# Attention kernel: q's norm factor given to the sigmoids as their scale, and the root's steps and all scaling of k on GpSimd

## The chip, the core and the metric

The kernel runs on one core of one Trainium2 chip. A core has five engines with a queue of instructions each: TensorE (PE in the profile; PEld is its weight load), VectorE (DVE), ScalarE (ACT), GpSimd (POOL) and SyncE (SP, which issues the DMAs here). An engine works its queue strictly in order; engines wait for one another through semaphores. The metric is the device time of one execution in microseconds; of several runs the median is taken.

## The reference

One block of an encoder on 1024 frames of 1024 features, all in float32: a SwiGLU feed-forward (half weight), stick-breaking attention, and a second SwiGLU. Only the attention is touched by the change.

```python
qkv = (xn @ w_qkv).reshape(b, s, 3, SB_HEADS, SB_HEAD_DIM)     # 16 heads of 64
q = rms_norm(qkv[:, :, 0], q_gain)...                          # over the 64 of a head
k = rms_norm(qkv[:, :, 1], k_gain)...
z = jnp.einsum('bhqd,bhkd->bhqk', q[:, :, lo:hi], k[:, :, :hi]) * scale      # scale = 1/8
log_beta = jax.nn.log_sigmoid(z)
log_1m = jnp.where(mask, jax.nn.log_sigmoid(-z), 0.0)
rev = lax.cumsum(log_1m, axis=3, reverse=True)                 # the keys between s and t
w = jnp.where(mask, jnp.exp(log_beta + rev_excl), 0.0)
outs.append(jnp.einsum('bhqk,bhkd->bhqd', w, v[:, :, :hi]))
```

`rms_norm` multiplies a head's 64 values of one frame by r = 1/sqrt(mean of squares + 1e-6) and by the gain. For q, r is one number for each frame and head, so it is one number for each row of z.

## The kernel before

Frames are stored in reverse order, so that the cumulative product runs forward. Matrix products are made of parts: every operand is split into a high part (rounded by ScalarE) and a low part (the rest, a subtraction), and three products are summed; this split is the helper on lines 159 and 160 and appears in the profile under these lines.

**Tiling.** The 16 heads are worked in 8 pairs. `qkv(p)` is a sequence of 8 steps, one for each block of 128 frames: a step makes q, k and v of a pair's two heads in one bank of PSUM (24 products of 128 x 384), copies q and k into a tile `qk`, takes squares and their sums (`ssq`), and splits v. After the fourth and the eighth step (a *half* of the frames: half 1 comes first, then half 0) the root r is found for 4 blocks x 4 (two q heads, two k heads) at once, in `rsqrt`: a first guess from the bits of the number and three rounds of Newton, on tiles of 128 x 16. Then q and k of that half are multiplied by r.

**Per head.** `prep` turns q and k of a half with PE transposes, puts in the gains and splits them (`q_s`, `kh_s`, `kl_s`). `weights` makes, for each block of 128 queries, z = q·k in banks of 512 keys (PE, lines 729 and 730), two sigmoids of each bank on ScalarE (`om`, line 731: sigmoid of -z; `w`, line 732: sigmoid of z; the factor 0.125 is the sigmoid's scale), a cleared first column (GpSimd, line 733), a scan that multiplies up `om` (VectorE, line 734), and the product of the two (line 735). `values` turns the weights back with PE transposes (line 756), splits them into `th` (ScalarE) and `tl` (VectorE), and multiplies them by v into the bank `bo` (lines 765 and 766); `o` is put together on lines 768 and 769. There are two `om` buffers, so that the sigmoids of a block wait until the product of line 735 two blocks before has read its `om`; there is one buffer of `w` for each block.

**Engines.** Which engine does an elementwise step is written in a set of names, `ON_POOL`: w0, w4 and w5 (the product of line 735 for query blocks 0, 4 and 5: 1023, 511 and 383 columns) are on GpSimd, the other five on VectorE; k of half 1 is scaled on GpSimd, k of half 0 and all of q on VectorE; of the four splits of a pair's qkv weights (`wql`, 128 x 768 each) three are on GpSimd and the second one on VectorE.

**Order.** The program is written in a fixed order (`PLAN`, a list of prep and use for head and half; `FILLS`, which says after which query block a qkv step of the *next* pair is put in; the values of a use come one use later), and a scheduler with priorities (`sooner`) turns it into one queue for each engine. So in a pair's stretch of the queues stand its own weights and values and the qkv steps of the next pair.

**Memory.** A kernel's tiles come from pools that are laid one after another in the order in which they are named; what follows the attention uses the same memory, so its loads and splits wait for the attention's tiles. Pool `sq` holds the squares, their sums and the root's tiles.

Of the kernel before, what the change touches and what calls it, by code (L numbers as in the profile page):

```python
# [9 lines left out]
F32 = mybir.dt.float32  # L10
# [3 lines left out]
ALU = mybir.AluOpType  # L14
# [20 lines left out]
ON_POOL = {  # L35
    "k1", "last w5", "last w7", "w0", "w4", "w5", "wo0", "wo1", "wo2", "wo3", "wql0", "wql2", "wql3", "xl0",
    "xl2", "xl3", "xl4",
}
# [59 lines left out]
def macaron_kernel(ctx, tc, x, g1, w1_in, w1_out, gm, w_qkv, gq, gk, w_o, g2, w2_in, w2_out, out):  # L98
# [8 lines left out]
    def lane(name):  # L107

        return pool_e if name in ON_POOL else dve
# [32 lines left out]
    def any_bank(tags=ROUND):  # L142
        turn[0] += 1
        return bank(tags[turn[0] % len(tags)])

    ident = cpool.tile([P, P], F32, name="ident")
    make_identity(nc, ident)

    below = cpool.tile([P, 16], F32, name="below")
    xh = cpool.tile([P, KD, T], F32R, name="xh")  # L150
# [7 lines left out]
    def split(raw, hi, lo, engine=None):  # L158
        act.activation(hi, raw, AF.Copy)  # L159
        (engine or dve).tensor_tensor(lo, raw, hi.bitcast(F32), op=ALU.subtract)  # L160

    def rsqrt(pool, ss, inv_n):

        shape = list(ss.shape)
        a = pool.tile(shape, F32, name="rs_a")
        u = pool.tile(shape, F32, name="rs_u")
        y = pool.tile(shape, F32, name="rs_y")
        dve.tensor_scalar(a, ss, inv_n, EPS, op0=ALU.mult, op1=ALU.add)
        dve.tensor_scalar(y.bitcast(I32), a.bitcast(I32), -0.5, -550020641.0, op0=ALU.mult, op1=ALU.add)
        for _ in range(3):  # L170
            dve.scalar_tensor_tensor(out=u, in0=y, scalar=0.5, in1=a, op0=ALU.mult, op1=ALU.mult)
            dve.tensor_tensor(u, u, y, op=ALU.mult)
            dve.scalar_tensor_tensor(out=y, in0=u, scalar=1.5, in1=y, op0=ALU.subtract, op1=ALU.mult)
        return y
# [445 lines left out]
    with pools(  # L620
        "raw_qkv", "wq1", "wq0", "wq2", "qk1", "qk0", "vst0", "sq", "vst1", "st1", "st0", "om", "w", "first", "th", "o"
    ) as pl:
# [9 lines left out]
        def qkv_weights(p):  # L632
            wh, wl = {}, {}
            for k0 in (4, 0) if p == 0 else (0, 4):
# [15 lines left out]
        def qkv(p, state):  # L650
# [3 lines left out]
            for half in (1, 0):  # L654
# [4 lines left out]
                for i, tb in enumerate(b4):  # L659
# [3 lines left out]
                    with sooner(OFF["e"]):  # L663
                        sq = pl["sq"].tile([P, 4, DH], F32, name="sq")
                        act.activation(qk[:, i, 0:2].rearrange("p a b -> p (a b)"), ps[:, :P], AF.Copy)
# [9 lines left out]
                        if i == 3:  # L675
                            r = rsqrt(pl["sq"], ssq.rearrange("p a b -> p (a b)"), 1.0 / DH)
# [3 lines left out]
                            lane(f"q{half}").tensor_tensor(qv, qv, rq, op=ALU.mult)  # L680
                            for hd in range(2):
                                kv = qk[:, :, 2 + 2 * hd : 4 + 2 * hd, :].rearrange("p a c b -> p a (c b)")
                                rk = r[:, :, 2 + hd : 3 + hd].to_broadcast([P, 4, P])
                                lane(f"k{half}").tensor_tensor(kv, kv, rk, op=ALU.mult)
                    yield
# [27 lines left out]
        def weights(state, hd, half, fill):  # L713

            w = []
            for tb in range(half * 4, half * 4 + 4):
                with sooner(OFF["w"]):
# [4 lines left out]
                    for kb in range(half, 2):  # L722
# [7 lines left out]
                        pe.matmul(z[:, : off + n], q, state["k", hd, kb][1][:, keys], start=False, stop=True)  # L730
                        act.activation(om[:, c0 : c0 + n], z[:, off : off + n], AF.Sigmoid, scale=-0.125)  # L731
                        act.activation(wt[:, c0 : c0 + n], z[:, off : off + n], AF.Sigmoid, scale=0.125)
                    pool_e.memset(wt[:, 0:1], 0.0)
# [196 lines left out]
```

## Time and profile before

| | |
|---|---|
| median of 3 runs | 2067.39 us (2066.3 to 2070.5) |
| the profiled execution's own time | 2066.78 us |
| its span, first to last instruction | 2064.9 us |
| granted TensorE clock, mean | 0.983 |
| busy in the span | PE 95%, PEld 80%, DVE 67%, ACT 47%, POOL 47% |
| the attention | from about 690 us to 1335 us of the span |
| a pair's period inside it | 75.3 us |

Busy shares are means over stages that have different limits: the two feed-forwards take some 1,420 us and the attention some 645 us. Only the attention's rows say what this change can do. In a timeline row the first two numbers are start and duration in us, and the bracket at the end tells how long the engine had been idle and what ended it. Times inside a pair repeat every 75.3 us, so one pair is read and then multiplied.

### The profile page before, as it was taken

How to read it: one execution, taken by the hardware profiler on the slowest of the kernel's cores; microseconds unless marked ns; L12 is line 12 of the kernel's file. 1: busy time of each engine (PE TensorE's matmuls, PEld its weight loads, DVE VectorE, ACT ScalarE, POOL GpSimd, SP SyncE). 2: the span in 40 equal slices, each digit the busy share in tenths (PEclk: the TensorE clock that was granted, in tenths of full speed). 3: DMA queues.
4: the chain of work that ended last, by engine and by line, in shares of the span. 5: the costliest groups of instructions: out<-in, count | busy, mean ns of one | idle time of the engine just before them, and what ended most of it. 6: DMA issues, size and time to landing. Idle time of an engine off the chain costs nothing.

```text
span 2064.9 us, 27122 instructions
## 1 busy us (share of the span) xinstructions
PE 1956.6 (95%) x9624; PEld 1649.9 (80%) x9624; DVE 1377.0 (67%) x1840; ACT 965.4 (47%) x1876; POOL 966.3 (47%) x772
## 2 busy tenths in 40 slices
PE   7899999999999989899899997899999999999999
PEld 6788888887887878777787785588888888888887
DVE  7845546447749688889888889638556455447754
ACT  6433433433335366667666666425333434434332
POOL 2567666655546132322322324102466666655554
PEclk9999999999999999999999997899999999999999
DMA  5223323249886111001001103322233232259974
GB/s 199 72 92 123 102 83 127 97 142 322 318 287 216 55 31 41 24 19 41 29 14 41 47 6 102 121 88 72 82 104 106 97 117 98 95 175 339 332 259 160
DMA packets 163031, 251.85 MB, mean 122 GB/s; under 512 B 10960, under 2 KB 80592, under 8 KB 162896
## 3 DMA queue, kind: packets, MB, share of 16 engines
q1 hardware_dynamic: 162896, 250.13, 35.3%
q8 instruction: 75, 1.23, 0.2%
q14 instruction: 60, 0.49, 0.1%
HBM read 193.99 MB, written 56.10 MB: 121 GB/s over the span
## 4 chain that ended last, share of the span: by engine, by line
PE 72%; DVE 18%; ACT 3%; issue 2%; POOL 2%; DMA 1%; ACTq 0%; DVEq 0%; POOLq 0%
PE ka L244 6%; PE ka L245 6%; PE ka L246 5%; DVE om L734 4%; PE kc L246 4%; PE kc L244 4%; PE kc L245 4%; PE kb L246 3%; PE kb L244 3%; PE kb L245 3%; PE ma L244 3%; PE ma L246 3%; PE ma L245 3%; PE mb L245 3%; PE mb L244 3%; PE mb L246 3%
## 5 line engine op out<-in xcount | busy, mean ns | idle before, releaser
L160 POOL TENSOR_TENSOR u<-sf,u 128x512 fp32r<-128x512 f32 x160 | 226.5, 1417 | 160.5 <-ACT u L159 159.7
L160 POOL TENSOR_TENSOR rp<-raw,rp 128x1024 fp32r<-128x1024 f32 x84 | 207.8, 2477 | 180.3 <-ACT rp L159 172.4
L160 POOL TENSOR_TENSOR u<-raw,u 128x512 fp32r<-128x512 f32 x136 | 198.7, 1464 | 142.3 <-ACT u L159 142.1
L159 ACT ACTIVATE u<-sf 128x512 fp32r<-128x512 f32 x160 | 100.9, 630 | 217.7 <-PE kb L245 89.8
L352 DVE TENSOR_TENSOR h<-h 128x512 f32<-128x512 f32 x110 | 134.9, 1228 | 87.1 <-POOL h L453 86.4
L734 DVE TENSOR_TENSOR_SCAN om<-om,first 128x512 f32<-128x512 f32 (+7 forms) x128 | 186.3, 1458 | 3.0 <-ACT om L731 2.6
L159 ACT ACTIVATE rp<-rh 128x1024 fp32r<-128x1024 f32 (+1 forms) x78 | 76.8, 984 | 210.9 <-issue 68.8
L244 PE MATMUL ka<-xh,u 128*128 128x512 f32 (+1 forms) x448 | 162.8, 364 | 8.2 <-ACT s L402 7.6
L245 PE MATMUL ka<-xl,u 128*128 128x512 f32 (+1 forms) x448 | 162.4, 363 | 1.2 <-DVE xl L160 1.2
L246 PE MATMUL ka<-xh,u 128*128 128x512 f32 (+1 forms) x448 | 162.0, 362 | 0.0
L159 ACT ACTIVATE u<-raw 128x512 fp32r<-128x512 f32 x136 | 84.8, 632 | 160.7 <-PE ka L245 102.1
L474 DVE TENSOR_TENSOR raw<-raw 128x1024 f32<-128x1024 f32 (+1 forms) x60 | 94.2, 1573 | 96.0 <-DMA raw<-w_out 88.9
L244 PE MATMUL bq<-wqh,xh 128*128 128x384 f32 x448 | 156.9, 350 | 0.0
L245 PE MATMUL bq<-wql,xh 128*128 128x384 f32 x448 | 155.1, 346 | 0.0
L246 PE MATMUL bq<-wqh,xl 128*128 128x384 f32 x448 | 154.0, 344 | 0.0
L244 PE MATMUL ma<-rp 128*128 128x512 f32 x352 | 137.4, 390 | 2.9 <-DVE h L406 2.9
L379 DVE TENSOR_TENSOR sf<-raw 128x512 f32<-128x512 f32 x80 | 79.1, 990 | 89.2 <-POOL u L160 89.1
L246 PE MATMUL ma<-rp 128*128 128x512 f32 x352 | 137.0, 389 | 0.0
L245 PE MATMUL ma<-rp 128*128 128x512 f32 x352 | 137.0, 389 | 0.0
L453 POOL TENSOR_TENSOR h<-h,g 128x512 f32<-128x512 f32 x80 | 111.0, 1387 | 36.4 <-DVE h L406 32.8
L159 ACT ACTIVATE th<-bt 128x512 fp32r<-128x512 f32 x192 | 94.5, 506 | 67.8 <-PE bt L756 63.3
L160 DVE TENSOR_TENSOR rp<-rh,rp 128x1024 fp32r<-128x1024 f32 (+1 forms) x70 | 108.8, 1568 | 24.9 <-ACT rp L159 22.6
(226 smaller groups left out, 5613.2 us busy)
## 6 DMA issues: line engine op xcount, KB each, us to landing
raw<-w_out SPq DMA_DIRECT2D x120, 512.0 KB, 5.2
raw<-w_in SPq DMA_DIRECT2D x88, 512.0 KB, 3.6
k<-h SPq DMA_DIRECT2D x154, 256.0 KB, 2.0
rh<-k SPq DMA_DIRECT2D x64, 512.0 KB, 6.0
raw_qkv<-w_qkv SPq DMA_DIRECT2D x64, 192.0 KB, 2.9
x_keep<-x SPq DMA_DIRECT2D x32, 256.0 KB, 3.4
x<-x_keep SPq DMA_DIRECT2D x32, 256.0 KB, 5.6
raw<-w_out SPq DMA_DIRECT2D x24, 256.0 KB, 4.1
```

The lines of the kernel that those rows point to most:

```text
L159: act.activation(hi, raw, AF.Copy)
L160: (engine or dve).tensor_tensor(lo, raw, hi.bitcast(F32), op=ALU.subtract)
L244: pe.matmul(dst, ah, bh, start=start and i == 0, stop=False, skip_group_check=onto)
L245: pe.matmul(dst, ah, bl, start=False, stop=False, skip_group_check=onto)
L246: pe.matmul(dst, al, bh, start=False, stop=stop and i == n - 1, skip_group_check=onto)
L352: dve.tensor_tensor(src, hb[of[0]], hb[of[1]], op=getattr(ALU, of[2]))
L379: dve.tensor_tensor(f[n], x, y, op=op)
L453: pool_e.tensor_tensor(h, h, gs[k], op=ALU.mult)
L474: dve.tensor_tensor(w[0], w[0], w[1], op=getattr(ALU, W_OF[m][2]))
L734: dve.tensor_tensor_scan(om[:, :L], om[:, :L], first[:, :L], initial=0.0, op0=ALU.mult, op1=ALU.max)
```

## The change

1. **q isn't scaled.** The product of q with r is left out. Two rows of factors, 0.125 r and -0.125 r, are made for each half (`f`, two small GpSimd instructions), and each of the two sigmoids takes its row's factor as a scale from memory in place of a constant. Before, q had to wait for r ahead of its transposes; now the sigmoids do.
2. **The root.** VectorE keeps the first two steps (`rs_a`, `rs_y`). The three rounds of Newton go to GpSimd, as 1 + 3 x 4 instructions on 128 x 16 (VectorE did a round in 3).
3. **k.** ScalarE copies q and k with one instruction where it used two, without writing each k head twice. GpSimd scales k for both halves: head 1 is written twice from one copy in one instruction of 512 columns, head 0 in two of 256.
4. **Weight splits.** All four `wql` splits of a pair are on GpSimd; the second one was on VectorE.
5. **Places in memory.** `f` makes the pool `sq` larger by 256 bytes per partition; the pool is named last, so that every other pool of the attention lies 2560 bytes, 5 x 512, lower than before or where it was. `below` (64 bytes) is laid ahead of the identity matrix, which so begins 64 bytes later.

The rows below are queue entries: source line (of the version it stands in), operation, output<-inputs, columns; `w` is the weights tile of a query block, told by its columns (511 is block 4, 383 block 5).

GpSimd, around the end of a pair, where half 0 of the next pair is scaled and the next pair's first weights begin; before:

```order
L160 TENSOR_TENSOR wql<-raw_qkv,wqh 128x768 x2
L733 MEMSET w_9810 128x1
L760 MEMSET th 128x128
L761 MEMSET tl 128x128
L160 TENSOR_TENSOR wql<-raw_qkv,wqh 128x768
L733 MEMSET w_9890 128x1
L735 TENSOR_TENSOR w_9890<-w_9890,om 128x511
L733 MEMSET w_9900 128x1
L735 TENSOR_TENSOR w_9900<-w_9900,om 128x383
```

And in the change, the same place from the last round's end (the twelve steps ahead of it, behind the first two `wql` splits, are left out):

```order
L746 MEMSET w_9840 128x1
L177 TENSOR_TENSOR rs_y<-rs_u,rs_y 128x16
L686 TENSOR_TENSOR qk_9526<-qk_9526,rs_y 128x4x128
L693 TENSOR_SCALAR f_9837<-rs_y 128x8 x2
L689 TENSOR_TENSOR qk_9526<-qk_9526,rs_y 128x4x64 x2
L773 MEMSET th 128x128
L159 TENSOR_TENSOR wql<-raw_qkv,wqh 128x768
L774 MEMSET tl 128x128
L159 TENSOR_TENSOR wql<-raw_qkv,wqh 128x768
L746 MEMSET w_9920 128x1
L748 TENSOR_TENSOR w_9920<-w_9920,om 128x511
L746 MEMSET w_9930 128x1
```

The thirteen steps, two `f`, three scalings of k and one more `wql` split now stand ahead of the product of block 4.

VectorE, some 30 us later, in the first weights of half 0 (query blocks 0, 1, 2: scans of 1024, 896, 768); before:

```order
L734 SCALAR_TENSOR_TENSOR om<-om,first 128x1024
L674 TENSOR_REDUCE ssq<-sq 128x4
L769 TENSOR_TENSOR o_7873<-bo,o_tmp 64x512
L673 TENSOR_TENSOR vst<-bq,vst 128x128
L160 TENSOR_TENSOR wql<-raw_qkv,wqh 128x768
L734 SCALAR_TENSOR_TENSOR om<-om,first 128x896
L673 TENSOR_TENSOR vst<-bq,vst 128x128
L735 TENSOR_TENSOR w_8441<-w_8441,om 128x895
L674 TENSOR_REDUCE ssq<-sq 128x4
L734 SCALAR_TENSOR_TENSOR om<-om,first 128x768
```

And in the change:

```order
L747 SCALAR_TENSOR_TENSOR om<-om,first 128x1024
L782 TENSOR_TENSOR o_8738<-bo,o_tmp 64x512
L679 TENSOR_REDUCE ssq<-sq 128x4
L678 TENSOR_TENSOR vst<-bq,vst 128x128
L747 SCALAR_TENSOR_TENSOR om<-om,first 128x896
L748 TENSOR_TENSOR w_9309<-w_9309,om 128x895
L678 TENSOR_TENSOR vst<-bq,vst 128x128
L679 TENSOR_REDUCE ssq<-sq 128x4
L747 SCALAR_TENSOR_TENSOR om<-om,first 128x768
```

The split between the scans of blocks 0 and 1 is gone from this queue (it is the last `wql` row of GpSimd's above).

GpSimd, in the second head's first weights, where half 1 of the next pair is scaled; before:

```order
L735 TENSOR_TENSOR w_10334<-w_10334,om 128x511
L684 TENSOR_TENSOR qk_10097<-qk_10097,rs_y 128x4x128 x2
L733 MEMSET w_10378 128x1
L735 TENSOR_TENSOR w_10378<-w_10378,om 128x383
L733 MEMSET w_10388 128x1
```

And in the change (five of the thirteen steps stand ahead of these rows):

```order
L746 MEMSET w_10367 128x1
L174 TENSOR_TENSOR rs_u<-rs_y,rs_a 128x16
L748 TENSOR_TENSOR w_10367<-w_10367,om 128x511
L175 TENSOR_TENSOR rs_u<-rs_u,rs_y 128x16
L176 TENSOR_SCALAR rs_u<-rs_u 128x16
L177 TENSOR_TENSOR rs_y<-rs_u,rs_y 128x16
L174 TENSOR_TENSOR rs_u<-rs_y,rs_a 128x16
L175 TENSOR_TENSOR rs_u<-rs_u,rs_y 128x16
L176 TENSOR_SCALAR rs_u<-rs_u 128x16
L177 TENSOR_TENSOR rs_y<-rs_u,rs_y 128x16
L686 TENSOR_TENSOR qk_10127<-qk_10127,rs_y 128x4x128
L693 TENSOR_SCALAR f_10364<-rs_y 128x8 x2
```

Behind them stand the two scalings of 256 columns and then the product of block 5 (383 columns).

The diff, without the moved names of the pools and of `below`:

```diff
 ON_POOL = {
-    "k1", "last w5", "last w7", "w0", "w4", "w5", "wo0", "wo1", "wo2", "wo3", "wql0", "wql2", "wql3", "xl0",
-    "xl2", "xl3", "xl4",
+    "last w5", "last w7", "w0", "w4", "w5", "wo0", "wo1", "wo2", "wo3", "xl0", "xl2", "xl3", "xl4",
 }
...
-    def rsqrt(pool, ss, inv_n):
+    def rsqrt(pool, ss, inv_n, e=dve):
...
+        if e is pool_e:
+            e.tensor_scalar(a, a, 0.5, None, op0=ALU.mult)
         for _ in range(3):
-            dve.scalar_tensor_tensor(out=u, in0=y, scalar=0.5, in1=a, op0=ALU.mult, op1=ALU.mult)
-            dve.tensor_tensor(u, u, y, op=ALU.mult)
-            dve.scalar_tensor_tensor(out=y, in0=u, scalar=1.5, in1=y, op0=ALU.subtract, op1=ALU.mult)
+            if e is pool_e:
+                e.tensor_tensor(u, y, a, op=ALU.mult)
+                e.tensor_tensor(u, u, y, op=ALU.mult)
+                e.tensor_scalar(u, u, 1.5, None, op0=ALU.subtract)
+                e.tensor_tensor(y, u, y, op=ALU.mult)
+            else:
+                e.scalar_tensor_tensor(out=u, in0=y, scalar=0.5, in1=a, op0=ALU.mult, op1=ALU.mult)
+                e.tensor_tensor(u, u, y, op=ALU.mult)
+                e.scalar_tensor_tensor(out=y, in0=u, scalar=1.5, in1=y, op0=ALU.subtract, op1=ALU.mult)
...
-                    split(raw, h_[:, ks], l_[:, ks], lane(f"wql{k // 2}") if p else pool_e)
+                    split(raw, h_[:, ks], l_[:, ks], pool_e)
...
-                        act.activation(qk[:, i, 0:2].rearrange("p a b -> p (a b)"), ps[:, :P], AF.Copy)
-                        pk = ps[:, P : 2 * P].rearrange("p (a b) -> p a b", b=DH)
-                        pk = pk.unsqueeze(2).to_broadcast([P, 2, 2, DH])
-                        act.activation(qk[:, i, 2:6].rearrange("p (a c) b -> p a c b", c=2), pk, AF.Copy)
                         act.activation(sq.rearrange("p a b -> p (a b)"), ps[:, : 2 * P], AF.Square)
+                        act.activation(qk[:, i, 0:4].rearrange("p a b -> p (a b)"), ps[:, : 2 * P], AF.Copy)
...
-                            qv = qk[:, :, 0:2, :]
-                            rq = r[:, :, 0:2].unsqueeze(3).to_broadcast([P, 4, 2, DH])
-                            lane(f"q{half}").tensor_tensor(qv, qv, rq, op=ALU.mult)
-                            for hd in range(2):
-                                kv = qk[:, :, 2 + 2 * hd : 4 + 2 * hd, :].rearrange("p a c b -> p a (c b)")
-                                rk = r[:, :, 2 + hd : 3 + hd].to_broadcast([P, 4, P])
-                                lane(f"k{half}").tensor_tensor(kv, kv, rk, op=ALU.mult)
+                            rk = r[:, :, 3:4].unsqueeze(3).to_broadcast([P, 4, 2, DH])
+                            kv = qk[:, :, 3:4, :].to_broadcast([P, 4, 2, DH])
+                            pool_e.tensor_tensor(qk[:, :, 4:6, :], kv, rk, op=ALU.mult)
+                            for to in (3, 2):
+                                rk = r[:, :, 2:3].to_broadcast([P, 4, DH])
+                                pool_e.tensor_tensor(qk[:, :, to, :], qk[:, :, 2, :], rk, op=ALU.mult)
+                            f = state["f", half] = pl["sq"].tile([P, 2, 4, 2], F32, name=f"f{half}")
+                            for n, c in enumerate((0.125, -0.125)):
+                                pool_e.tensor_scalar(f[:, n], r[:, :, 0:2], c, None, op0=ALU.mult)
...
-                        act.activation(om[:, c0 : c0 + n], z[:, off : off + n], AF.Sigmoid, scale=-0.125)
-                        act.activation(wt[:, c0 : c0 + n], z[:, off : off + n], AF.Sigmoid, scale=0.125)
+                        for to, sign in ((om, 1), (wt, 0)):
+                            act.activation(
+                                to[:, c0 : c0 + n], z[:, off : off + n], AF.Sigmoid,
+                                scale=f[:, sign, tb % 4, hd : hd + 1],
+                            )
```

More of the change, by code (lines that the diff above doesn't have):

```diff
@@ L144, in any_bank @@
         return bank(tags[turn[0] % len(tags)])
+    below = cpool.tile([P, 16], F32, name="below")
     ident = cpool.tile([P, P], F32, name="ident")
     make_identity(nc, ident)
-    below = cpool.tile([P, 16], F32, name="below")
     xh = cpool.tile([P, KD, T], F32R, name="xh")
@@ L620, in macaron_kernel @@
     with pools(
-        "raw_qkv", "wq1", "wq0", "wq2", "qk1", "qk0", "vst0", "sq", "vst1", "st1", "st0", "om", "w", "first", "th", "o"
+        "raw_qkv", "wq1", "wq0", "wq2", "qk1", "qk0", "vst0", "vst1", "st1", "st0", "om", "w", "first", "th", "o", "sq"
     ) as pl:
@@ L675, in qkv @@
                         if i == 3:
-                            r = rsqrt(pl["sq"], ssq.rearrange("p a b -> p (a b)"), 1.0 / DH)
+                            r = rsqrt(pl["sq"], ssq.rearrange("p a b -> p (a b)"), 1.0 / DH, pool_e)
                             r = r.rearrange("p (a b) -> p a b", b=4)
-                            qv = qk[:, :, 0:2, :]
-                            rq = r[:, :, 0:2].unsqueeze(3).to_broadcast([P, 4, 2, DH])
-                            lane(f"q{half}").tensor_tensor(qv, qv, rq, op=ALU.mult)
-                            for hd in range(2):
-                                kv = qk[:, :, 2 + 2 * hd : 4 + 2 * hd, :].rearrange("p a c b -> p a (c b)")
-                                rk = r[:, :, 2 + hd : 3 + hd].to_broadcast([P, 4, P])
-                                lane(f"k{half}").tensor_tensor(kv, kv, rk, op=ALU.mult)
+                            rk = r[:, :, 3:4].unsqueeze(3).to_broadcast([P, 4, 2, DH])
[7 more added lines that the diff above has]
+                                pool_e.tensor_scalar(f[:, n], r[:, :, 0:2], c, None, op0=ALU.mult)
                     yield
@@ L715, in weights @@
             w = []
+            f = state["f", half]
             for tb in range(half * 4, half * 4 + 4):
```

## The prediction

> **What bounds the kernel now.** First the busy time of stretches inside the attention, 70 us each; the columns are start and end, PE, PEld, DVE, ACT, POOL, then the granted clock.
>
> ```profile
> 830.00:900.00 70.00, 64.66 (x373) 56.30 (x373) 60.49 (x100) 44.95 (x110) 21.68 (x34) 1.00 0.10 31
> 970.00:1040.00 70.00, 63.15 (x356) 54.70 (x355) 59.60 (x99) 43.29 (x110) 20.46 (x32) 0.98 0.10 31
> 975.00:980.00 5.00, 3.34 (x18) 2.39 (x17) 4.90 (x8) 3.19 (x10) 0.10 (x1) 0.97 0.07 19
> 980.00:985.00 5.00, 5.00 (x25) 4.90 (x24) 2.81 (x5) 1.25 (x3) 0.41 (x2) 0.69 0.00 0
> ```
>
> TensorE is the bound with 64 of 70 us, VectorE follows with 60, and GpSimd has 70% to spare. So relief of VectorE pays only at the few places where TensorE waits for it. After the wait at 975 to 980 the clock granted falls to 0.69 for 5 us, which loses another 0.31 x 5 = 1.5 us. The second view is TensorE's timeline over one pair; the bracket is its wait.
>
> ```profile
> 943.94 0.50 PE L766 MATMUL bo<-tl,vst 128*128 128x512 f32 x1 [0.69 <-DVE tl L160]
> 947.81 0.41 PE L729 MATMUL bz<-kh_s,q_s 128*128 128x384 f32 x1 [0.46 <-DVE q_s L700]
> 950.14 0.38 PE L766 MATMUL bo<-tl,vst 128*128 128x256 f32 x1 [0.65 <-DVE tl L160]
> 955.30 0.47 PE L765 MATMUL bo<-th,vst 128*128 128x512 f32 x1 [1.59 <-DVE o L769]
> 979.23 0.51 PE L766 MATMUL bo<-tl,vst 128*128 128x512 f32 x1 [1.66 <-DVE tl L160]
> 995.05 0.50 PE L766 MATMUL bo<-tl,vst 128*128 128x512 f32 x1 [0.86 <-DVE tl L160]
> 1002.11 0.50 PE L766 MATMUL bo<-tl,vst 128*128 128x512 f32 x1 [0.44 <-DVE tl L160]
> ```
>
> All are waits for VectorE. Place one, a pair's end, holds 0.69 + 0.46 + 0.65 + 1.59 = 3.39 us; place two, the first weights of half 0, 1.66 + 1.5 for the clock; place three, where half 1 is scaled, 0.86 + 0.44 = 1.30. Together 7.85 us a pair. The stage from 740 to 1250 us holds 510 / 75.3 = 6.8 pairs, so 53 us is all that relief of VectorE can bring.
>
> **What leaves VectorE.** Groups of 735 to 1330 us (busy us and mean ns stand behind the bar):
>
> ```profile
> L171 DVE SCALAR_TENSOR_TENSOR rs_u<-rs_y,rs_a 128x16 f32<-128x16 f32 x42 | 22.2, 529 | 0.9
> L173 DVE SCALAR_TENSOR_TENSOR rs_y<-rs_u,rs_y 128x16 f32<-128x16 f32 x42 | 13.2, 315 | 0.9
> L172 DVE TENSOR_TENSOR rs_u<-rs_u,rs_y 128x16 f32<-128x16 f32 x42 | 8.7, 207 | 0.7
> L160 DVE TENSOR_TENSOR wql<-raw_qkv,wqh 128x768 fp32r<-128x768 f32 x6 | 11.4, 1902 | 0.0
> L684 DVE TENSOR_TENSOR qk<-qk,rs_y 128x512 f32<-128x512 f32 x15 | 11.3, 788 | 0.0
> L680 DVE TENSOR_TENSOR qk<-qk,rs_y 128x512 f32<-128x512 f32 x14 | 10.0, 716 | 0.5
> ```
>
> That is 76.8 us over 14 halves or 7 pairs, 11 us a pair. But the steps of 16 columns need not last 529 ns:
>
> ```profile
> 913.72 1.28 POOL L735 TENSOR_TENSOR w<-w,om 128x511 f32<-128x511 f32 x1 [0.69 <-DVE rs_y L169]
> 913.74 1.29 DVE L171 SCALAR_TENSOR_TENSOR rs_u<-rs_y,rs_a 128x16 f32<-128x16 f32 x1
> 915.07 0.17 DVE L172 TENSOR_TENSOR rs_u<-rs_u,rs_y 128x16 f32<-128x16 f32 x1
> 952.40 0.95 DVE L734 TENSOR_TENSOR_SCAN om<-om,first 128x384 f32<-128x384 f32 x1
> 952.49 1.91 POOL L735 TENSOR_TENSOR w<-w,om 128x511 f32<-128x511 f32 x1 [1.46 <-DVE rs_u L172]
> ```
>
> A step takes 0.17 us alone. The one at 913.74 took 1.29 and ended with GpSimd's product of 913.72; conversely the product of 1.28 us took 1.91 when a scan had begun 0.09 us ahead of it. The two engines keep one another out, and who came first goes first. The Trainium skill has this as a rule ("SBUF — State Buffer", Who interferes with whom): a VectorE operation with two inputs in SBUF and a GpSimd operation that reads SBUF contend for an exclusive lock. The trace agrees by the rows above. So a step that moves to GpSimd trades its time on VectorE for waits behind scans, and bars VectorE while it runs.
>
> **What it costs on GpSimd.**
>
> ```profile
> L735 POOL TENSOR_TENSOR w<-w,om 128x127 f32<-128x127 f32 x2 | 0.9, 452 | 1.2 <-DVE om L734 1.2
> 916.78 3.21 POOL L684 TENSOR_TENSOR qk<-qk,rs_y 128x512 f32<-128x512 f32 x2 [1.78 <-DVE rs_y L173]
> 947.89 1.84 POOL L160 TENSOR_TENSOR wql<-raw_qkv,wqh 128x768 fp32r<-128x768 f32 x1 [2.32 <-ACT wqh L159]
> ```
>
> Products of 511 columns in 1.28 and of 127 in 0.452 give 2.16 ns a column and 0.18 us ahead; 16 columns are then 0.21 us (an estimate by the line through the two), and 13 steps 2.7 us. Below nothing it can't go, and 13 x 0.452 = 5.9 is the upper bound. k of a half costs 3.2 us at most (3.21 stands above for the same 2 x 512 columns) and 2.2 at least (2 x 512 columns by the line, 2 x 1.28 at most); the two `f` 0.4.
>
> *Place two.*
>
> ```profile
> 969.19 2.40 POOL L735 TENSOR_TENSOR w<-w,om 128x1023 f32<-128x1023 f32 x1 [2.02 <-ACT w L732]
> 970.32 2.09 DVE L160 TENSOR_TENSOR wql<-raw_qkv,wqh 128x768 fp32r<-128x768 f32 x1
> 972.33 2.01 DVE L734 TENSOR_TENSOR_SCAN om<-om,first 128x896 f32<-128x896 f32 x1
> 978.50 0.68 DVE L160 TENSOR_TENSOR tl<-bt,th 128x512 fp32r<-128x512 f32 x1
> ```
>
> The weight split leaves VectorE here. Its 2.09 us aren't won whole: the product on GpSimd ends at 969.19 + 2.40 = 971.59, and a scan of two SBUF inputs waits that long. It starts at 971.59 instead of 972.33, 0.74 us earlier, and so does everything behind it to `tl` at 978.50, for which TensorE waits 1.66. I take 0.74 and half of the clock's loss: -1.5 us a pair. Bounds: -3.2 (wait and dip go) and 0.
>
> *Place three.* VectorE loses the steps and the q scaling from 913.74 on (to 916.74 + 0.69, 3.7 us); the waits of 1.30 can go. Against it stands the GpSimd queue: thirteen steps, `f`, k and then the product of block 5.
>
> ```profile
> 916.74 0.69 DVE L680 TENSOR_TENSOR qk<-qk,rs_y 128x512 f32<-128x512 f32 x1
> 920.00 1.34 POOL L735 TENSOR_TENSOR w<-w,om 128x383 f32<-128x383 f32 x1
> ```
>
> Before, that product ended at 921.34. Now rows start at 913.72: the product of 511 (1.28), 2.7 + 0.4, k 2.2 to 3.2 and 1.0 to 1.3 for 383 columns end at 921.3 to 922.6 with no scan in the way. Scans of 384 and 256 columns fall there, at most 0.95 each (the row of 952.40 has 384). I take 0.6 from the middle of that and 0.4 for collisions, +1.0 of delay, against -1.3: -0.3 a pair; bounds -1.3 and, with 1.3 and both scans of delay, 3.2 - 1.3 = +1.9.
>
> *Place one.*
>
> ```profile
> 943.81 0.16 DVE L169 TENSOR_SCALAR rs_y<-rs_a 128x16 int32<-128x16 int32 x1
> 945.33 1.48 DVE L734 TENSOR_TENSOR_SCAN om<-om,first 128x640 f32<-128x640 f32 x1
> 950.09 0.81 DVE L735 TENSOR_TENSOR w<-w,om 128x639 f32<-128x639 f32 x1
> 951.20 1.21 DVE L734 TENSOR_TENSOR_SCAN om<-om,first 128x512 f32<-128x512 f32 x1
> 954.43 0.38 ACT L731 ACTIVATE om<-bz 128x256 f32<-128x256 f32 x1 [1.11 <-POOL w L733]
> ```
>
> The guess is there at 944.0. GpSimd then needs 2.7 + 0.4 + 2.2 to 3.2, then two splits of 1.84 and the product of 1.28: it ends at 954.3 to 955.3 without collisions, where it ended at 952.49 + 1.91 = 954.40. But the scans of 945.33, 951.20 and 952.40 and the product of 950.09 (1.48 + 1.21 + 0.95 + 0.81 = 4.45 us in all) bar the chain; between none and all I take half, so the product comes 0.4 + 2.2 = 2.6 us later. ScalarE's sigmoid at 954.43 waits for that product already, since there are two `om`, and behind it in its queue are `th` and the next head's sigmoids. VectorE without its steps can bring all of -3.4; against it +2.6: -0.8 a pair; bounds -3.4 and 0.4 + 4.5 - 3.4 = +1.5.
>
> Sum of the places: -1.5 - 0.3 - 0.8 = -2.6 a pair, x 6.8 = -17.7 us.
>
> *ScalarE.*
>
> ```profile
> L731 ACT ACTIVATE om<-bz 128x512 f32<-128x512 f32 x95 | 58.9, 621 | 8.6 <-PE bz L730 5.9 <-POOL w L735 2.0
> L699 ACT ACTIVATE kh_s<-bz,gk_sb 128x512 fp32r<-128x512 f32 x30 | 20.9, 696 | 7.2 <-PE bz L695 6.9
> L665 ACT ACTIVATE qk<-bq 128x128 f32<-128x128 f32 x55 | 15.4, 280 | 61.6 <-PE bq L246 60.5
> ```
>
> The second row has its scale from memory, the first a constant, both from PSUM with 512 columns: +75 ns. A pair has 2 heads x 12 banks x 2 sigmoids = 48: +3.6 us, and 8 copies of 0.28 fewer: -2.2; net +1.4. ScalarE is 64% busy in the first row of windows, so I charge half: +0.7 x 6.8 = +4.8, bounds 0 and +9.5. The last pair, which has no next pair's copies to save: half of 3.6, +1.8. By the Trainium skill ("ScalarE: Activation LUTs", What ACT_TABLE_LOAD costs) an operand of one column adds about 93 ns: 4.5 us a pair in place of 3.6, which would move the sum by 0.45 x 6.8 = 3 us; the trace's pair of rows decides for 75.
>
> *Ends.* In the tail the feed-forward's loads and splits no longer stand behind as many of the attention's tiles: 1.2 us earlier at most, taken as -1.2.
>
> ```profile
> 737.26 1.12 PE L695 MATMUL bz<-ident,qk 128*128 128x128 f32 x4 [1.70 <-DVE kl_s L700]
> ```
>
> In the prologue the first pair's k waits for thirteen steps on GpSimd, but q no longer for any; I take 0, within 2. Places modulo 512 stay as they were for all tiles that stream; nothing in the trace prices such a move of `ident`, and I take 0.
>
> **Sum:** -17.7 + 4.8 + 1.8 - 1.2 = -12.3 on the execution's 2066.78 (span 2064.9 and 1.9 around it): 2054.5. The median of the runs stands 0.6 above that execution: 2055.
>
> **Rivals.**
>
> *The GpSimd queue becomes the wait* (slower). Its point is the products of blocks 4 and 5. With all collisions, the upper bounds above, place one costs +1.5 and place three +1.9; place two brings only its 0.74. So (1.5 + 1.9 - 0.74) x 6.8 = +18, with ScalarE and the ends (4.8 + 1.8 - 1.2 = 5.4) +23: 2091. It decides once the two delays together pass 5.4 us a pair: I charge 2.6 + 1.0 = 3.6, and 12.3 / 6.8 = 1.8 more eats the gain. From there to 2091 the middle is 2079. For it: the wait at 954.43 is there already, and ScalarE's queue carries it on. Against: GpSimd idles 70%, and VectorE loses 11 us that barred it as well. The Trainium skill ("Perfetto Trace Analysis", Optimizing Scalar/DVE Operations) speaks for it too, in warning that moving work between GPSIMD and DVE might not help since they share a port.
>
> *Full relief.* The products on GpSimd come no later, all seven waits and half of the dip's 1.5 go: -7.1 x 6.8 + 5.4 = -43: 2024; with place one's 1.59 left, 2035. Middle 2030. For it: 11 us leave, and 7.85 are waited. Against: the lock rows.
>
> *Nothing comes of it.* TensorE's queue is full; the relief lands where nothing waits, or VectorE's gain goes to locks: 2064 to 2071. For it: the windows' 64 of 70 us.
>
> **How the numbers follow.** The forecast 2055 has 0.48. Half way to their bounds the places add in squares to sqrt(0.85^2 + 0.5^2 + 1.3^2) = 1.6 us a pair below and sqrt(0.75^2 + 1.1^2 + 1.15^2) = 1.8 above, x 6.8 11 and 12 us; its own range is 2044 to 2063, where no change begins. The others: the GpSimd queue 0.30, full relief 0.08, nothing 0.14. What a measurement here can tell from no change is 0.2%, 4 us. Faster: 0.48 + 0.08, less 0.02 of the forecast's upper edge = 0.54; same 0.15; slower 0.31. The range 2036 to 2084 leaves out most of full relief and a third of the slower case, 0.15 to 0.2 together.
>
> **What would show it.** Right: a pair's period, 75.3 us by the rows of place one, falls to about 73; the waits for `tl` at place two shrink below 1 us; the sigmoids take 75 ns more; the steps on GpSimd take 0.2 us with a few of 1 us. Wrong: ScalarE's waits for the products of 511 and 383 columns grow above 2 us, GpSimd's steps take 0.5 us on average, or TensorE's waits move to another line with the same sum. A sum that comes right from other places (the clock, the prologue) would also make the working wrong.

## The result, and the profile after

The changed kernel takes 2115.2 us (median of 4 runs, 2113.7 to 2118.2) against 2068.9 for the kernel before (4 runs): a ratio of 1.0224, 95% interval 1.0203 to 1.0246. It is slower by 46 us, where 12 us less were forecast; it lies 24 us above the worst that the rivals allowed.

The profiled execution's span is 2114.6 us, 49.7 more. GpSimd's product of block 0 with 1023 columns marks a place in a pair; these are timeline rows of GpSimd, of before and of after, at the start of the second pair and five pairs later.

```profile
819.72 2.41 POOL L735 TENSOR_TENSOR w<-w,om 128x1023 f32<-128x1023 f32 x1 [2.02 <-ACT w L732]
1194.02 2.40 POOL L735 TENSOR_TENSOR w<-w,om 128x1023 f32<-128x1023 f32 x1 [2.02 <-ACT w L732]
```
```profile
832.15 2.40 POOL L748 TENSOR_TENSOR w<-w,om 128x1023 f32<-128x1023 f32 x1 [1.93 <-ACT vst L677]
1238.93 2.40 POOL L748 TENSOR_TENSOR w<-w,om 128x1023 f32<-128x1023 f32 x1 [1.93 <-ACT vst L677]
```

Five pairs took 374.3 us and take 406.8: 32.5 us more, 6.5 a pair. All up to 832.15, which is the first pair and what stands ahead of it, is 12.4 us late; some 5 us come after the last of these rows, most of it behind the attention. So the loss is made in every pair, and one pair can be read for all. TensorE's waits of 0.4 us or more in one pair of after, from its timeline:

```profile
943.38 0.79 PE L778 MATMUL bo<-th,vst 128*128 128x512 f32 x1 [4.17 <-ACT th L158]
966.76 0.50 PE L779 MATMUL bo<-tl,vst 128*128 128x512 f32 x1 [1.25 <-DVE tl L159]
971.33 0.41 PE L739 MATMUL bz<-kh_s,q_s 128*128 128x384 f32 x1 [0.69 <-DVE q_s L709]
976.02 0.58 PE L778 MATMUL bo<-th,vst 128*128 128x256 f32 x1 [3.20 <-POOL th L773]
977.93 0.58 PE L779 MATMUL bo<-tl,vst 128*128 128x256 f32 x1 [1.33 <-POOL tl L774]
1004.53 0.50 PE L779 MATMUL bo<-tl,vst 128*128 128x512 f32 x1 [0.40 <-DVE tl L159]
```

Place two, the last row, is mended: 0.40 where it was 1.66. Place three (943) has one wait of 4.17 where two made 1.30, and place one (966 to 978) has 6.47 where it had 3.39. Two of its waits name GpSimd, which TensorE waited for nowhere in a pair before. And the clock, in the view by windows (columns as in the prediction; the last but two is the clock):

```profile
943.00:948.00 5.00, 4.62 (x15) 4.14 (x16) 3.75 (x4) 2.69 (x5) 0.00 (x0) 0.50 0.00 0
948.00:953.00 5.00, 4.99 (x29) 4.16 (x28) 1.59 (x4) 2.67 (x6) 0.55 (x4) 0.98 0.00 0
977.00:982.00 5.00, 4.07 (x17) 4.07 (x18) 2.34 (x2) 3.43 (x7) 4.02 (x6) 0.50 0.43 123
982.00:987.00 5.00, 5.00 (x36) 4.47 (x35) 4.75 (x10) 3.90 (x9) 1.15 (x3) 0.96 0.26 87
```

Behind each of the two stalls the clock is halved for some 5 us: 15 matmuls in 5 us at 943, 29 in the next 5. Summed over windows of 1.25 us as (1 - clock) x PE busy, the clock takes 4.9 us a pair, against 1.7 before in the pairs that have a dip. Not every pair of before has one: the pair from 819.72 loses nothing to the clock and takes 74.2 us, while the three behind it lose 1.7 each and take 75.3, so by this comparison a dip counted as 1.7 us costs a pair 1.1. What holds TensorE at 976 is seen on GpSimd (timeline of after):

```profile
966.20 0.26 POOL L171 TENSOR_SCALAR rs_a<-rs_a 128x16 f32<-128x16 f32 x1 [0.33 <-DVE rs_y L168]
966.55 0.22 POOL L174 TENSOR_TENSOR rs_u<-rs_y,rs_a 128x16 f32<-128x16 f32 x1
966.85 0.22 POOL L175 TENSOR_TENSOR rs_u<-rs_u,rs_y 128x16 f32<-128x16 f32 x1
...
968.10 1.39 POOL L175 TENSOR_TENSOR rs_u<-rs_u,rs_y 128x16 f32<-128x16 f32 x1
969.58 0.94 POOL L176 TENSOR_SCALAR rs_u<-rs_u 128x16 f32<-128x16 f32 x1
...
971.84 0.22 POOL L177 TENSOR_TENSOR rs_y<-rs_u,rs_y 128x16 f32<-128x16 f32 x1
972.14 1.05 POOL L686 TENSOR_TENSOR qk<-qk,rs_y 128x512 f32<-128x512 f32 x1
973.16 1.38 POOL L693 TENSOR_SCALAR f<-rs_y 128x8 f32<-128x8 f32 x2
974.51 1.31 POOL L689 TENSOR_TENSOR qk<-qk,rs_y 128x256 f32<-128x256 f32 x2
975.76 0.20 POOL L773 MEMSET th<- 128x128 f32 x1
975.93 1.80 POOL L159 TENSOR_TENSOR wql<-raw_qkv,wqh 128x768 fp32r<-128x768 f32 x1
977.67 0.20 POOL L774 MEMSET tl<- 128x128 f32 x1
977.83 1.81 POOL L159 TENSOR_TENSOR wql<-raw_qkv,wqh 128x768 fp32r<-128x768 f32 x1
979.97 1.27 POOL L748 TENSOR_TENSOR w<-w,om 128x511 f32<-128x511 f32 x1
```

The clearings of `th` and `tl`, 0.2 us each, come behind the root, k, the factors and a weight split; TensorE multiplies by these tiles 0.06 us after each is cleared. At place three ScalarE is in between (its timeline, after):

```profile
941.63 0.37 ACT L742 ACTIVATE om<-bz,f 128x128 f32<-128x128 f32 x1 [4.54 <-POOL w L746]
941.90 0.36 ACT L742 ACTIVATE w<-bz,f 128x128 f32<-128x128 f32 x1
942.15 0.69 ACT L742 ACTIVATE om<-bz,f 128x512 f32<-128x512 f32 x1
942.72 0.61 ACT L158 ACTIVATE th<-bt 128x512 fp32r<-128x512 f32 x1
```

The sigmoid at 941.63 waits for GpSimd's product of block 5 (940.61 to 941.60) to give back one of the two `om`; the releaser is shown as the clearing of `w` right behind that product. `th`, for which TensorE stands from 939.2 on, is three instructions further down ScalarE's queue.

### The profile page after: what moved, and what is told of

Read it like the earlier page. It is cut to its first block, busy times and chain, and to the rows that moved or that the text cites. A ratio compares the mean times of both kernels' runs of the same rounds, so it can differ in the third digit from the quotient of the medians.

```text
span 2114.6 us, 27202 instructions
## 1 busy us (share of the span) xinstructions
PE 1969.1 (93%) x9624; PEld 1669.6 (79%) x9624; DVE 1328.2 (63%) x1657; ACT 987.8 (47%) x1812; POOL 1075.0 (51%) x1051
## 5 line engine op out<-in xcount | busy, mean ns | idle before, releaser
L747 DVE TENSOR_TENSOR_SCAN om<-om,first 128x512 f32<-128x512 f32 (+7 forms) x128 | 192.8, 1508 | 48.0 <-ACT om L742 47.5
L254 PE MATMUL bq<-wqh,xl 128*128 128x384 f32 x448 | 159.0, 355 | 0.0
L742 ACT ACTIVATE om<-bz,f 128x512 f32<-128x512 f32 (+1 forms) x192 | 113.9, 595 | 60.4 <-POOL w L746 40.8
L778 PE MATMUL bo<-th,vst 128*128 128x512 f32 x192 | 83.0, 432 | 57.5 <-ACT th L158 32.2
```

Of the source, the lines that this page charges most:

```text
L254: pe.matmul(dst, al, bh, start=False, stop=stop and i == n - 1, skip_group_check=onto)
L742: act.activation(to[:, c0 : c0 + n], z[:, off : off + n], AF.Sigmoid, scale=f[:, sign, tb % 4, hd : hd + 1],)
L747: dve.tensor_tensor_scan(om[:, :L], om[:, :L], first[:, :L], initial=0.0, op0=ALU.mult, op1=ALU.max)
L778: pe.matmul(ot[:, :n], vv, th[:, :n], start=sb == NT - 1, stop=False)
```

## Experiments

Theory: TensorE stalls because small things that ScalarE or TensorE waits for stand on GpSimd behind the root's chain. Rivals: the load itself, by the mutual exclusion of VectorE and GpSimd; the longer sigmoids; the places in memory. All ratios are against the kernel before.

| run | median us | ratio, 95% interval | pair, us | of it clock, us |
|---|---|---|---|---|
| before | 2068 to 2069 | | 75.3 | 1.7 |
| the change | 2115.2 | 1.0203 to 1.0246 | 81.7 | 4.9 |
| e1, product 5 on VectorE | 2095.1 | 1.0097 to 1.0154 | 78.5 | 2.0 |
| e2, clearings on VectorE | 2113.8 | 1.0189 to 1.0243 | 82.0 | 4.3 |
| e3, both | 2095.3 | 1.0099 to 1.0167 | 79.9 | 2.1 |
| e4, scale from memory alone | 2075.6 | 1.0018 to 1.0047 | 75.7 | 0.8 |
| e5, e3 and product 4 | 2079.5 | 1.0037 to 1.0067 | 77.2 | 2.3 |
| e6, root on VectorE | 2082.3 | 1.0050 to 1.0100 | 76.8 | 2.3 |
| e7, before + split | 2069.8 | 0.9994 to 1.0015 | 75.0 | 0.8 |
| e8, e5 + root on VectorE | 2072.4 | 1.0012 to 1.0031 | 75.7 | 1.6 |
| e9, before + q's factor | 2073.6 | 1.0009 to 1.0035 | 74.8 | 0.0 |
| e10, before + places | 2068.4 | 0.9994 to 1.0013 | | |
| e11, change, sq in old place | 2118.2 | 1.0229 to 1.0258 | | |
| e12, before, k and splits for products | 2067.0 | 0.9981 to 1.0004 | 75.3 | 0.0 |
| e13, change, one round | 2068.5 | 0.9983 to 1.0007 | 74.6 | 0.8 |
| e14, e9 + e7 | 2075.6 | 1.0020 to 1.0046 | 75.6 | 1.7 |
| e15, e14, products on VectorE | 2071.5 | 1.0004 to 1.0022 | 75.6 | 0.9 |

The pair is a mean over two pairs of the profiled execution, between rows as above; the clock is summed as above, over the same two pairs, and for the kernel before over pairs with a dip. A pair's length varies by up to 1.1 us within one execution (74.2 to 75.3 in the kernel before), so the pair is no verdict; the ratio is.

**The two waits taken away (e1, e2, e3).**

```diff
-    ... "w0", "w4", "w5", ...        # e1, e3
+    ... "w0", "w4", ...
-  pool_e.memset(th[:, P : 2 * P].bitcast(F32), 0.0)      # e2, e3; tl likewise
+  dve.memset(th[:, P : 2 * P].bitcast(F32), 0.0)
```

> The changed kernel with one edit: the product of query block 5 (383 columns) is VectorE's and not GpSimd's. Queue theory (ScalarE's sigmoids wait for an om buffer that this product frees, and it stands on GpSimd behind the root, the factors and the scaling of k): TensorE's wait of 4.17 us for th at the place where half 1 is scaled falls to under 1 us and the clock dip behind it goes, 3.2 + about 2 us a pair, x 6.8 = -35: about 2080 us. Lock theory (the loss is spread over many small exclusions between VectorE and GpSimd): the product only changes its engine, 2105 to 2115 us. Sigmoid theory (ScalarE's longer sigmoids carry the loss): no change, 2115 us.

> The changed kernel with one edit: the two clearings of th and tl (128 x 128) are VectorE's and not GpSimd's. Queue theory: TensorE's waits of 3.20 and 1.33 us at a pair's end, which name these clearings, go, and the dip behind them; 4.5 + about 2 us a pair, x 6.8 = -44, less what comes late next (the product of block 4, behind two weight splits): 2075 to 2095 us. Lock theory: 2105 to 2115 us. Sigmoid theory: 2115 us.

> Both edits together. Queue theory: the two stalls are at different places and add up: 2040 to 2065 us, at or below the kernel before. Lock theory: 2100 us or more. Sigmoid theory: 2110 to 2115 us, as ScalarE has the same work.

e1 gained 20 us of the 35 expected. The wait of 4.17 is gone; in its place stand two for `tl`, as in the kernel before (TensorE's timeline, e1):

```profile
938.10 0.50 PE L779 MATMUL bo<-tl,vst 128*128 128x512 f32 x1 [0.81 <-DVE tl L159]
942.61 0.50 PE L779 MATMUL bo<-tl,vst 128*128 128x512 f32 x1 [0.72 <-DVE tl L159]
970.34 0.58 PE L778 MATMUL bo<-th,vst 128*128 128x256 f32 x1 [3.19 <-POOL th L773]
```

e2 gained nothing, and e3 nothing over e1; e3 is 30 us above the slow end of what was expected. The clearings no longer hold TensorE, but the next entry of the same queue does, the product of block 4, through ScalarE. GpSimd's and ScalarE's timelines and TensorE's, of e2:

```profile
982.28 4.23 POOL L159 TENSOR_TENSOR wql<-raw_qkv,wqh 128x768 fp32r<-128x768 f32 x2
986.50 1.25 POOL L748 TENSOR_TENSOR w<-w,om 128x511 f32<-128x511 f32 x1
987.79 0.47 ACT L742 ACTIVATE om<-bz,f 128x256 f32<-128x256 f32 x1 [5.28 <-POOL w L746]
989.17 0.80 PE L778 MATMUL bo<-th,vst 128*128 128x512 f32 x1 [4.54 <-ACT th L158]
```

And ScalarE's and TensorE's of e3, where the same product comes at 972.75; TensorE's transpose waits there for a bank that the sigmoids have yet to read:

```profile
974.04 0.47 ACT L742 ACTIVATE om<-bz,f 128x256 f32<-128x256 f32 x1 [5.59 <-POOL w L746]
974.93 0.47 PE L704 MATMUL bz<-ident,qk 128*128 128x128 f32 x1 [5.39 <-ACT w L742]
```

The stall at place one belongs to the queue and not to the clearing: whichever entry behind the chain is wanted first carries it.

**The rest of the queue emptied, and the root taken back (e5, e6, e8).** e5 is e3 with `"w4"` taken out as well; e6 is the change with `rsqrt(..., 1.0 / DH)`, without its last argument; e8 is both.

> The run with both edits, and block 4's product (511 columns) on VectorE too, so that nothing that ScalarE or TensorE waits for stands behind GpSimd's root but the scaled k and the factors. Queue theory: the 5.4 us wait at a pair's end that followed the two edits (for the sigmoids that wait for the om of block 4) goes with its dip: 79.4 - 5.4 - 1 to 2 = about 73 us a pair, 2040 to 2060 us. Rival, VectorE's load: the three products (2.3 us a head) are back on VectorE, which then is the wait at every tl: 2075 us or more.

> The changed kernel with the root's three rounds back on VectorE, in three steps a round; the factors, k and the splits stay on GpSimd. Queue theory: GpSimd's chain ahead of the products is 4 to 5 us shorter, which is the length of the stalls: a pair of 74 to 77 us, 2055 to 2080 us. If the scaling of k and the extra split are enough to hold the products up: 2090 us or more.

> As the fifth run, and the root on VectorE as well: GpSimd has only k, the factors, the splits and block 0's product. Queue theory alone: no GpSimd wait is left, 2045 to 2065 us. VectorE's load: the root's 18 steps and the products are all there, tl is late everywhere, 2070 us or more. Against the fifth run it prices the root on VectorE once no queue stands behind it.

e5 is 16 us better than e3, and 2079.5, not the 2040 to 2060 of the queue theory: the rival of VectorE's load was right about its size. Part of what is left is the exclusion (e5, VectorE and GpSimd timelines):

```profile
964.22 2.32 DVE L747 TENSOR_TENSOR_SCAN om<-om,first 128x384 f32<-128x384 f32 x1
```
```profile
963.91 4.24 POOL L159 TENSOR_TENSOR wql<-raw_qkv,wqh 128x768 fp32r<-128x768 f32 x2
```

A scan that took 0.95 us in the kernel before takes 2.32 beside the two splits, and `tl` behind it is what TensorE waits 2.0 us for. What the rest of e5's 11 us over the kernel before is made of was not taken apart; e4 below prices the longer sigmoids at some 6.5 of them. e6 puts the price on the root's rounds: with them back on VectorE the change is 33 us faster, 2 us above its expected range, and no other work changed its engine. e8 is 7 us under e5 though VectorE has the root too, and again misses the range of the queue theory alone and meets that of VectorE's load. GpSimd is the worse place for the root even where, of what others wait for, only k and the factors stand close behind it. No run moves the root alone in the kernel before.

**The chain made shorter (e13).**

```diff
-        for _ in range(3):
+        for _ in range(1 if e is pool_e else 3):
```

> The changed kernel with one round of Newton in place of three in the attention's roots (the roots are then less exact): eight of GpSimd's thirteen small steps a half are gone, everything else stays in its order. Queue theory: the product of block 5 and the clearings come 8 x 0.3 to 0.4 = 2.4 to 3.4 us earlier, so of the stalls of 4.17 and 3.20 about 1 us and 0 to 0.8 are left, and the dips go: -5.5 to -8 us a pair, x 6.8, 2060 to 2078 us. If it is the load on GpSimd and not who waits behind it: 70 us of steps go down to 27, of which little is on TensorE's path: 2100 us or more.

The queues of TensorE, VectorE and ScalarE are the same row by row; in GpSimd's, eight steps a half are gone and block 4's product changes places with a few steps beside it. The steps take 23.0 us instead of 70.3 over 14 halves, 3.4 us a half less, and the kernel gains 47 us, 6.7 a pair: twice 3.4. A pair's waits of TensorE, e13:

```profile
951.98 0.50 PE L779 MATMUL bo<-tl,vst 128*128 128x512 f32 x1 [1.24 <-DVE tl L159]
957.28 0.41 PE L739 MATMUL bz<-kh_s,q_s 128*128 128x384 f32 x1 [1.40 <-DVE q_s L709]
959.66 0.39 PE L779 MATMUL bo<-tl,vst 128*128 128x256 f32 x1 [0.78 <-POOL tl L774]
965.48 0.51 PE L778 MATMUL bo<-th,vst 128*128 128x512 f32 x1 [0.99 <-ACT th L158]
1004.58 0.50 PE L778 MATMUL bo<-th,vst 128*128 128x512 f32 x1 [1.16 <-ACT th L158]
```

The stalls of 4.17 and 3.20 are 1.16 and below 0.4, and the clock's loss fell from 4.9 to 0.8 us. Of the runs this is the one that settles it, since nothing was moved to another engine. It also speaks against the exclusion as the cause, since that did not shrink: over the attention (735 to 1330 us) the scan of 640 columns takes 1.80 us on average where it took 1.49 in the change, and a scaling of 256 columns on GpSimd 1.02 where it took 0.62.

**The parts alone (e4, e7, e9, e10, e11).** e4: the kernel before, sigmoids with `scale=eighth[:, 1:2]`, a tile that holds the constants. e7: the kernel before, with all `wql` on `pool_e`. e9: the kernel before, with `f` in place of q's scaling. e10: the kernel before, with pool `sq` last and `below` first. e11: the change, with `sq` back in its old place, behind `vst0`.

> The kernel before with the sigmoids' scale read from memory (two columns that hold 0.125 and -0.125) in place of a constant, and pool sq named last and larger, as in the change; q is still scaled on VectorE. Queue theory: the sigmoids take 70 to 85 ns more, but ScalarE isn't the bound: 2067 to 2080 us. Sigmoid theory: 48 x 0.08 us a pair, x 6.8 = +26, half of the loss or more: 2090 to 2095 us. If places in memory matter by themselves, it shows here too.

> The kernel before with one edit: the second weight split of a pair is GpSimd's too. From the profile after (the wait of 1.66 us at the first weights of half 0 became 0.40, and the dip there went): 1.3 + 1.5 us a pair, x 6.8 = -19: 2050 us, 2060 by the 0.74 us of the prediction alone. If the gain at that place was owed to other parts of the change: 2067 us.

> The kernel before with the change's first part alone: q isn't scaled, the two rows of factors are made on GpSimd (two small instructions a half), the sigmoids take them as scale; the root, k and the splits stay where they were. VectorE loses 0.7 us a half, ScalarE's sigmoids take 80 ns more. By the run with the scale from memory alone (+6.5 us) and a gain of at most 1.4 us a pair, x 6.8 = 9.5: 2065 to 2076 us. If q's factor on the path of the sigmoids (they must wait for the root and f, where q's transposes did) is a wait of its own: 2080 us or more.

> The kernel before with the change's places alone: pool sq named last and the 64 bytes of the mask laid ahead of the identity. The engines' queues inside the pairs are the same row by row. Queue theory and the prediction: within 4 us of the kernel before. If places matter (the identity feeds every transpose): several us either way, and the rest of the loss must be counted from there.

> The changed kernel with pool sq named where it stood, so that the factors' 256 bytes shift the later tiles by half of 512. Queue theory: the same queues, the same stalls, 2110 to 2120 us. If the place modulo 512 bytes matters to the streams of these tiles, it shows as a change of several us, spread over all rows that read them.

The scale from memory costs 6.5 us in all. With q's product gone as well (e9) it is 4.6; the intervals overlap, so what the product was worth isn't told apart from nothing. The split alone (e7) is within the measurement: place two gained 0.63 us, and TensorE waits 1.05 elsewhere (its timeline, e7).

```profile
954.87 0.33 PE L756 MATMUL bt<-ident,w 128*128 128x128 f32 x1 [1.05 <-DVE w L735]
982.51 0.50 PE L766 MATMUL bo<-tl,vst 128*128 128x512 f32 x1 [1.03 <-DVE tl L160]
```

The expected 2050 to 2060 is a miss. Places cost nothing that can be measured: e10 is 0.03% from before, and e11 3 us from the change, with intervals that overlap.

**Is there a better kernel in it (e12, e14, e15)?** e12: the kernel before with `"k0"` and all `wql` on GpSimd, `"w4"` and `"w5"` off it. e14: e9 with all `wql` on GpSimd. e15: e14 without `"w4"` and `"w5"`.

> The kernel before with k of half 0 and the second split moved to GpSimd and, in exchange, the products of blocks 4 and 5 to VectorE; constants as the sigmoids' scale, q and the root on VectorE. Queue theory: nothing that ScalarE waits for stands on GpSimd behind anything but other products, so 2050 to 2068 us, the best of these. VectorE's load: it gives 1.36 + 1.9 us a pair away and takes four products, 2.3 us, so it can gain no more than the locks give back: 2062 to 2075 us.

> The kernel before with the parts of the change that cost little apart, q's factor as the sigmoids' scale and the second split on GpSimd, together; root and k as before. From their pairs (74.8 and 75.0 us against 75.3): 74.5 to 75 us a pair; 2062 to 2072 us, so at best 0.3% under the kernel before.

> As the run ahead, with the products of blocks 4 and 5 on VectorE, so that no sigmoid waits for GpSimd beyond the first column's clearing: 2060 to 2070 us if those waits (25.8 us over seven pairs in the kernel before) were on the path, 2070 to 2080 us if VectorE's 2.3 us a pair are.

None is faster beyond its interval; e12 at 2067.0 equals the kernel before. e14's median is above its expected range and lies further from before than e9's and e7's together, but the intervals overlap, so this is not told apart from their sum; e15 falls where VectorE's load was expected to put it. e9's profiled pair looks shorter than before's (74.8 against 75.3 us) though its median is longer. Its pairs lost nothing to the clock, and the pair of before that loses nothing is the one of 74.2: like with like, e9's is 0.6 us longer, which over 6.8 pairs is an estimate of 4 us, near the 4.6 measured.

## Why the prediction was wrong, step by step

**The bound** was read rightly: TensorE, with VectorE behind it. The step that failed is the next one: "relief of VectorE" was taken as a gain to be netted against lateness on GpSimd, and of the entries that stand behind the root on GpSimd only the two products were asked after.

| a pair, us | forecast | waits measured | clock | sum |
|---|---|---|---|---|
| place two | -1.5 | 1.66 to 0.40 | -1.7 | -3.0 |
| place three | -0.3 | 1.30 to 4.17 | +2.4 | +5.3 |
| place one | -0.8 | 3.39 to 6.47 | +2.5 | +5.6 |
| sum | -2.6 | | | +7.9 |

The period grew by 6.4. Of the other 1.5 us, 0.5 lie in shorter waits: all of TensorE's waits in a pair grew from 6.8 to 11.0, by 4.2 and not by the 4.7 of these rows. The last 1.0 most likely lies in the clock's column, which counts every slowed matmul, while the pair does not pay for all of them: in e7, pairs with 1.6 us of such loss and pairs with none are both 75.0 us long.

**Place two** came out near its lower bound, further than the working had it: the split alone took 0.63 us from this wait (e7), where the sum had 0.74, and the dip behind it was gone there too; but a new wait of 1.05 stands at place one, in some pairs with a dip of its own, and in all it brought nothing. So the mechanism held, but the 3 us in the change are not to be booked as the split's.

**Place three is where the netting failed.** Counted from the end of block 4's scan, in the rows of VectorE and ScalarE before, and of VectorE and GpSimd after,

```profile
912.41 1.22 DVE L734 TENSOR_TENSOR_SCAN om<-om,first 128x512 f32<-128x512 f32 x1
921.70 0.61 ACT L159 ACTIVATE th<-bt 128x512 fp32r<-128x512 f32 x1
```
```profile
930.42 1.23 DVE L747 TENSOR_TENSOR_SCAN om<-om,first 128x512 f32<-128x512 f32 x1
940.61 0.99 POOL L748 TENSOR_TENSOR w<-w,om 128x383 f32<-128x383 f32 x1
```

the product of block 5 ended 7.7 us later before (921.34) and ends 9.95 later now: 2.2 us of delay where "+1.0" was taken, inside the bound of 3.2. Part of it is that five root steps stand ahead of block 4's product, which the sum started at its old place. Another 0.8 came from ScalarE's queue: a sigmoid of 512 columns (0.57 to the next start) now stands ahead of `th`, and the two small ones ahead are longer. So `th` came 3.0 us later (it starts 8.1 us after that scan before, and 11.1 now), and TensorE, ready 0.9 us earlier since `tl` was no longer late, waited for all of it. Relief ahead of the late chain counts for nothing: TensorE goes on when the last of the two is there. The sum had -1.3 + 1.0; it should have been +3.0 by the chain alone.

**Place one lacked a wait.** The sum asked only when block 4's product comes. That came 15.1 us after the guess against 10.4 (954.40 and 981.24 against 943.97 and 966.11): +4.7, near the upper bound of 4.9, not the 2.6 taken. But before it stands what the rows of the order showed and the sum passed over, the two clearings between the splits. TensorE waits for them directly, 3.20 + 1.33. And the relief of 3.4 that was set against it came only in part: the 1.59 for `o` is gone, but `tl` and `q_s` cost 1.25 + 0.69 where the three waits of this kind cost 1.80.

**The step of 0.21 us** was right for a step by itself (0.22), and wrong for a chain: each needs the one before, and the starts are 0.30 to 0.35 us apart (966.20, 966.55, 966.85), so 13 steps take 4 us where nothing collides (an estimate from these starts), not 2.7. With the collisions of 968.10 and 969.58, which fall on VectorE's scan of 640 columns at 967.98 and its product at 969.57, they took 5.9. That is the number of the upper bound, but by luck: the bound had 0.45 for every step, and here two steps hold 2.3 of it. k took 2.3 us a half (14.7 + 18.0 over 14), near the lower bound of 2.2, the factors 0.9 where 0.4 stood.

**The dip was charged for the stall that went, and not for the stalls that came.** Two halvings of the clock make 4.9 us a pair. The rival that came true, the GpSimd queue, had 2091 as its far end; it lacked these 3.2 us more a pair, 22 us in 6.8 pairs, and these bring it to 2113. That this is so near the 2115 measured is in part luck: its waits added up to 2.7 us a pair (1.5 + 1.9 - 0.74) where the three places have 4.7, and the clock's loss is not paid in full. The sign named for it came: ScalarE's wait for the product of block 5 went from 2.54 to 4.54 us. Its chance of 0.30 looks too low: the rows of the order already showed three entries that others wait for with more ahead of them in an in-order queue.

**ScalarE** was right in size: 75 ns forecast, 703 against 621 ns, so 82 measured (from one start to the next 0.57 against 0.48 us). What of it lies on the path was too high: e4, which keeps the copies, paid 6.5 us for 48 x 0.08 x 7 = 27 us of longer sigmoids, a quarter and not the half that was charged. **Places**: nothing, as forecast (e10). **Ends**: -1.2 was forecast, and the part behind the last `o` is 4.1 us longer in this execution, 735.3 against 731.2; over all the profiled executions it runs from 729.8 to 737.4 us, and what sets it was not studied. What stands ahead of the first product of block 0 on GpSimd (it starts at 747.51 against 745.72) is 1.8 us longer, inside the 2 that were allowed; the first pair is 10.6 us longer (84.6 against 74.0), with 6.7 us of clock loss against 1.6, and why it loses more than the others is open.

## What to carry to other kernels

When a long chain goes to an idle in-order engine, list every entry that now stands behind it and who waits for that entry, the 0.2 us ones too: share of busy time says nothing about it, and moving one of them away can end its stall (e1) or only hand it to the next (e2, e3). Do not net relief on one engine against lateness on another; ask which of the two inputs is last. And look at the clock behind a new stall of TensorE: here each of the two slowed its matmuls by some 2.5 us more, though not all of that showed in the pair's length.

## What the runs showed of the hardware

The granted clock went to exactly 0.50 at TensorE's stalls of 4.17 and 3.20 us (the windows at 943 and 977) and was back some 5 us behind them. Counted in windows of 0.5 us, each of these two dips lasts 6.8 us, and the dips of the kernel before (at 904.5 and 979.7) 3.4. The Trainium skill ("TensorE: Matmul & The Clock Gate", Part 1: The HAM clock gate) says that the clock has two states, half and full, that a window of about 3.4 us without work halves it and a busy window restores it. The 0.50 and the lengths, one and two such windows, agree; but the kernel before has its dip behind a single wait of 1.66 us, shorter than such a window, so here less idle time was enough. Nor does the wait alone decide it: behind this one, in the pair of before that has no dip (TensorE's timeline), the clock stayed whole.

```profile
829.76 0.50 PE L766 MATMUL bo<-tl,vst 128*128 128x512 f32 x1 [1.65 <-DVE tl L160]
```

Dependent steps on GpSimd of 16 columns start 0.30 us apart while each is shown as 0.22 us busy; at 933.12 (after) a step is followed 0.18 us later by the product of block 4, which does not need it. With the collisions over the whole attention, three of the four kinds of step average 0.36 to 0.43 (groups of 735 to 1360 us, after):

```profile
L174 POOL TENSOR_TENSOR rs_u<-rs_y,rs_a 128x16 f32<-128x16 f32 x42 | 9.3, 223 | 3.2
L175 POOL TENSOR_TENSOR rs_u<-rs_u,rs_y 128x16 f32<-128x16 f32 x42 | 17.4, 415 | 2.7
L176 POOL TENSOR_SCALAR rs_u<-rs_u 128x16 f32<-128x16 f32 x42 | 18.2, 432 | 3.7
L177 POOL TENSOR_TENSOR rs_y<-rs_u,rs_y 128x16 f32<-128x16 f32 x42 | 15.3, 363 | 3.3
```
